# Two of four recurrent mixers take a block's 512 tokens at once; outputs after all states

## The chip, the core and the metric

The kernel runs on one core of a Trainium2 chip. The metric is the device time of one execution, in microseconds (us), lower is better. Each core has a matrix engine, TensorE (PE in the rows; PEld is its loading of weights, which overlaps the matmuls), the elementwise engines VectorE (DVE), ScalarE (ACT) and GpSimd (POOL), and SyncE (SP), which issues the DMA transfers here. PSUM is the memory that TensorE writes, SBUF the one that it reads.

## The reference

Two layers of a decoder. Each layer projects its input (2048 prompt tokens of width 1024, and 64 sample tokens that ride along) into four head groups, runs a recurrence in each, projects back, and adds a cross-attention into 256 memory tokens. Three of the groups (retention, HGRN2 and GLA) share one recurrence, in the reference's words:

```python
# S_t = diag(exp g_t) S_{t-1} + k_t v_t^T,  o_t = S_t^T q_t
o, s_ret  = chunked_gated_linear(q, k, v, log gamma, st['ret'])     # retention, 4 heads, 64 x 64 state
o, s_hgrn = chunked_gated_linear(silu(q), k_h, i, log_f, st['hgrn']) # HGRN2,     4 heads, 64 x 64
o, s_gla  = chunked_gated_linear(q, k, v, log_a, st['gla'])          # GLA,       4 heads, 32 x 64
o, S_rwkv = rwkv7_scan(r, w, k, v, kk, a, s0)                        # RWKV-7
out = concatenate([o_ret, o_hgrn, o_gla, o_rwkv]) @ w_out
```

Each group's output is normalised per head and gated with silu(g). The outputs are the tokens after both layers, the final states, and the memory keys and values.

## The kernel before

**Tiling.** The 2048 prompt tokens are four blocks b of TB = 512 tokens, each of NT = 4 tiles of 128. The eight steps (l,b) of two layers run one after the other in `block()`; the samples ride in b = 0 (`smp`), with their own mixers placed in blocks 0 and 1 (`TURN`).

**One block.** In program order: the projections of RWKV; `R_rwkv` in two halves of 256 tokens (PSUM lanes `psa` and `psc`); the projections of GLA, then `R_gla` in two halves (lane `psb`); the projections of HGRN, then `R_hgrn` in two halves (lane `psb`); the projections of retention, then `R_ret` in two halves (`psa`, `psc`). After it `gates()` multiplies with silu(g) (`th`, line 1266), and `finish()` does the output projection, the cross-attention and, with the next block's tokens, the normalisation and its transposes (`xs`, line 430, matmuls psb<-fpack,xs). Dense matmuls, those against the 1024-wide weights, write to lane `psd`; their weights come in 1 MB pieces into a ring `whl` of three. Weights that are still raw come through a ring `wrp` of three (tag "w", tiles `wraw`), which is in use in blocks 0 and 1 and idle in 2 and 3. Every PSUM lane has two buffers.

**A gated-linear mixer.** `dyadic()` builds the scores inside a tile of 128 tokens level by level, s = 1, 2, 4, 8, 16, 32, 64. At each level `products()` is a run of small matmuls of q against k on `psb`, whose results DVE puts into the score tile `sT` (line 736, a copy under a mask); then DVE scales k (`k_step`) and q (`q_step`) by the decays so far, and POOL forms the next decays `tot`. In GLA, where two heads share 64 partitions, q is held twice, masked (`qx`). `totok()` transposes the decayed k to tokens (`gmn` in GLA, `ha` in HGRN, `rkd` is retention's). `outputs()` then goes tile by tile: the query against the state (psb<-S_gla,qx), the scores against v (psb<-dn_gv,sT), the sum of kᵀv (psb<-dn_gv,gmn), and the update of the state in place on DVE (line 624); only then the next tile. At its end the whole output `osb` is normalised (`head_norm`) and transposed (psa or psc <-fpack,osb).

**Order.** Each engine runs its list in order. The list is made from priorities by program order, with an offset for each named part (`PRI`, so `wk2`, the GLA mixer, is pulled 223 ahead); `held()` keeps matmuls together, 12 dense ones or 48 others, before another lane may come between. So on TensorE dense runs stand between the small runs of the mixers, and whatever dense work is still unread covers the mixers' waits for DVE; late in a block none is left.

A program's small fp32 matmul is recorded twice in the trace: x16 in an order listing is x32 in a timeline row.

Of the kernel before, what the change touches and what calls it, by code (L numbers as in the profile page):

```python
# [22 lines left out]
TB = 512  # L23
# [110 lines left out]
def decoder(ctx, tc, I, C, O):  # L134
# [5 lines left out]
    NH = 4  # L140
# [422 lines left out]
    class Seg:  # L563
        def __init__(self, sample):
            self.sample = sample
            self.P = SN if sample else 128
            self.nt = 1 if sample else 2
            self.n = self.P * self.nt
            self.levels = SLEVELS if sample else LEVELS
# [26 lines left out]
    def outputs(seg, sT, at, v, qd, S, NG, NC, kT, tot, wp, eps, center, evac, state_out=None):  # L596
# [5 lines left out]
        if not seg.sample:  # L602
            po = PS("r").rearrange("p (t n) -> p t n", t=2)
            p5 = po.rearrange("p t (c g j d) -> p t c g j d", c=NC, g=2, j=NP)
            es = [slice(0, 64), slice(64, 128)]
            for t in range(nt):
                for c in range(NC):
                    for j in range(NP):
                        for e in es:
                            mm(p5[e, t, c, :, j, :], qd[:, c, j, t * 128 + e.start:t * 128 + e.stop], S[:, c, :], True, False)  # L610
                        for g in range(2):
                            h = c * NG + g * NP + j
                            x = sT[:, at(t, h)].rearrange("p e n -> p (e n)")
                            for e in es:
                                mm(po[e, t, h * 64:(h + 1) * 64], x[:, e], v[:, t, h * 64:(h + 1) * 64], False, True)
                pu = PS("r")[:, :NC * 64].rearrange("p (c n) -> p c n", c=NC)
                for h in range(NH):
                    c, g = divmod(h, NG)
                    mm(pu[g * KD:(g + 1) * KD, c, :], kT[:, t, h * KD:(h + 1) * KD], v[:, t, h * 64:(h + 1) * 64])
                for c in range(NC):  # L620
                    for p in range(2):
                        gs = slice(64 * p, 64 * p + 64)
                        blk = S[gs, c, p * 64:(p + 1) * 64]
                        V.scalar_tensor_tensor(blk, blk, tot(t, c)[gs], pu[gs, c, :], ALU.mult, ALU.add)
            tags = ("rqT", "rkT", None) if center else ("qx2", "qx2", 2)
            o = wp.tile([128, 2, 256], F32, name="osb", tag=tags[0], bufs=tags[2])
            A.activation(o, po, AF.Copy)
            head_norm(o, 128, 2, eps, center, wp, tags[1:], evac)
# [30 lines left out]
    def place(NG, NC, nt):  # L659

        NP = NG // 2

        def at(t, h):
            c, g = divmod(h, NG)
            p, j = divmod(g, NP)
            return ((p * nt + t) * NC + c) * NP + j
        return at

    def dyadic(seg, q, k, a, NG, NC, sT, wp):
# [10 lines left out]
        mine = lambda x, p: x[:, p * w:(p + 1) * w]  # L680

        def apart(i):
            if NP == 1:
                return q.unsqueeze(2)
# [6 lines left out]
        def products(s, f):  # L691
# [10 lines left out]
            for p in range(2):  # L702
                yield (mine(sT[:P], p)[:, :, 0, :].rearrange("p u (b f s) -> p u b f s", f=2, s=s)[:, :, :, f, :],
# [7 lines left out]
        def q_step(s, tot, x):  # L711
# [5 lines left out]
            new = wp.tile([128, NC, n // (2 * s)], F32, name=f"tot{s}", tag=f"tot{s}")  # L717
# [9 lines left out]
        tt(V, q, q, a, ALU.mult)  # L727
        tot = q_step(1, a, q.unsqueeze(2))
        Q[0] = apart(1)
        for li, s in enumerate(seg.levels):  # L730
# [6 lines left out]
            else:  # L737
                A.activation(sT[64:128, :, 1, :], sT[64:128, :, 0, :], AF.Copy)
                G.memset(sT[64:128, :, 0, :], 0.0)
                ps = [PS("r")[:, :NC * NP * 64].rearrange("p (c g n) -> p c g n", c=NC, g=NP) for _ in range(2)]  # L740
                for c in range(NC):
                    for t in range(nt):
                        for p in range(2):
                            mm(ps[p][64 * t:64 * t + 64, c], k[rows[p], c, t * P:t * P + 64], Q[0][rows[p], c, :, t * P + 64:t * P + 128])
                for t in range(nt):
                    for p in range(2):
                        o = mine(sT[0:64], p)[:, t * NC * NP:(t + 1) * NC * NP, 1, :]
                        A.activation(o, ps[p][64 * t:64 * t + 64].rearrange("p c g n -> p (c g) n"), AF.Copy)
# [4 lines left out]
        return Q[0], tot  # L753
# [18 lines left out]
    def gain(on, col):  # L772
        def f(ps):
            A.activation(on, ps, AF.Copy, scale=col)
        return f

    def plain(on):
        def f(ps):
            A.activation(on, ps, AF.Copy)
        return f  # L780

    def R_gla(l, seg, st, d, on, wp):
        c = cols[l]
        n = seg.n
        qk, v, sm = d["qk"], d["v"], d["sm"]
# [12 lines left out]
        sT = wp.tile([128, seg.nt * NH, seg.P // 64, 64], F32, name="sT", tag="sT")  # L798
        qd, tot = dyadic(seg, qk[:, 0:1, :], qk[:, 1:2, :], a, 4, 1, sT, wp)
        at = place(4, 1, seg.nt)  # L800
        kT = totok(qk[:, 1:2, :], 1, seg, wp, "gmn", 128)
        if seg.sample:
# [4 lines left out]
            outputs(seg, sT, at, v, qk[:, 0:1, :], S, 4, 1, kT, decay, wp, 32 * RMS_EPS, False,  # L807
                    gain(on, c["gla_norm"][:, 0:1]), lambda: sample_state_out(S, O[7][l], 32))
        else:
            outputs(seg, sT, at, v, qd, st, 4, 1, kT, lambda t, cc: tot[:, cc, t:t + 1], wp, 32 * RMS_EPS, False,  # L810
# [1211 lines left out]
```

## Time and profile before

| | |
|---|---|
| runs | 3624.22, 3611.39, 3616.11 us; median 3616.11 us |
| the profiled execution | 3606.43 us, its span 3604.6 us, so 1.8 us around it |
| mean granted TensorE clock | 0.968 of full |
| busy | PE 3366.3 us (93%), DVE 2112.9 (59%), ACT 1274.3 (35%), POOL 553.0 (15%) |
| idle time of PE in front of its matmuls | 227.8 us in all |

The profiled execution is 9.7 us under the median. The page's first part gives the busy time of each engine as a share of the span. The chain of waits starts at the last instruction and goes back to whatever released each step. The table of waits gives, for one engine, what it waited for, the total, the number of times and the longest. The timeline merges consecutive instructions of one kind into a row: its start, its length, how many, and in brackets the idle time ahead with what ended it. As matmuls are pipelined, the cost of a run in such a row is better read from the start of the next row than from its own length.

### The profile page before, as it was taken

How to read it: one execution, taken by the hardware profiler on the slowest of the kernel's cores; microseconds unless marked ns; L12 is line 12 of the kernel's file. 1: busy time of each engine (PE TensorE's matmuls, PEld its weight loads, DVE VectorE, ACT ScalarE, POOL GpSimd, SP SyncE). 2: the span in 40 equal slices, each digit the busy share in tenths (PEclk: the TensorE clock that was granted, in tenths of full speed). 3: DMA queues.
4: the chain of work that ended last, by engine and by line, in shares of the span. 5: the costliest groups of instructions: out<-in, count | busy, mean ns of one | idle time of the engine just before them, and what ended most of it. 6: DMA issues, size and time to landing. Idle time of an engine off the chain costs nothing.

```text
span 3604.6 us, 85661 instructions
## 1 busy us (share of the span) xinstructions
PE 3366.3 (93%) x36138; PEld 2835.7 (79%) x36138; DVE 2112.9 (59%) x6047; ACT 1274.3 (35%) x2729; POOL 553.0 (15%) x680
## 2 busy tenths in 40 slices
PE   7998799998999999999999997999889999999998
PEld 5877688886978888888877866878678888878887
DVE  5677545675436754576446765467644567446754
ACT  4442334422243324332344332443213333244323
POOL 3323231020000100011122242111100011000100
PEclk9999899998999999999999997999989999999999
DMA  6522565235662254324453255542445522542255
GB/s 191 184 98 89 180 218 192 77 112 163 200 215 90 82 196 150 135 76 173 170 172 121 83 155 175 197 153 94 136 153 186 176 98 92 188 160 103 76 195 188
DMA packets 241957, 530.79 MB, mean 147 GB/s; under 512 B 66854, under 2 KB 179750, under 8 KB 197542
## 3 DMA queue, kind: packets, MB, share of 16 engines
q1 hardware_dynamic: 241574, 525.31, 42.5%
q8 instruction: 285, 4.67, 0.5%
q14 instruction: 98, 0.80, 0.1%
HBM read 410.10 MB, written 115.16 MB: 146 GB/s over the span
## 4 chain that ended last, share of the span: by engine, by line
PE 75%; DVE 12%; ACT 5%; issue 3%; DMA 3%; POOL 2%; SPq 0%; POOLq 0%; ACTq 0%; DVEq 0%
PE psd L221 39%; PE psc L221 13%; PE psa L221 11%; PE psb L221 6%; PE psa L263 2%; PE psb L263 2%; PE psc L263 2%; DVE rsq L227 1%; DMA wraw<-in_w_in 1%; POOL whl L227 1%; DVE osb L227 1%; DVE hri L283 1%; DVE hss L552 1%; DVE dn_hq L227 0%; DMA whl<-w_low 0%
## 5 line engine op out<-in xcount | busy, mean ns | idle before, releaser
L221 PE MATMUL psd<-act,whl 128*128 128x512 f32 (+1 forms) x4032 | 1008.5, 402 | 28.6 <-DVE th L1266 12.8
L221 PEld LDWEIGHTS psd<-act,whl 128*128 128x128 f32 (+1 forms) x4032 | 741.4, 189 | 203.5 <-DVE th L1266 15.3
L221 PE MATMUL psd<-whl,act 128*128 128x256 f32 x3840 | 541.4, 292 | 7.0 <-POOL whl L227 3.3
L221 PEld LDWEIGHTS psd<-whl,act 128*128 128x128 f32 x3840 | 482.9, 193 | 28.6 <-issue 9.2
L227 POOL TENSOR_TENSOR whl<-wraw,whl 128x1024 fp32r<-128x1024 f32 (+1 forms) x90 | 218.0, 2428 | 383.3 <-ACT whl L349 366.2
L271 POOL TENSOR_TENSOR ri<-ri,mhalf 128x1 f32<-128x1 f32 (+1 forms) x87 | 50.6, 582 | 1103.9 <-DVE ri L270 1065.3
L221 PE MATMUL psd<-whl,oh 128*128 128x256 f32 x1152 | 211.4, 284 | 0.0
L221 PEld LDWEIGHTS psd<-whl,oh 128*128 128x128 f32 x1152 | 177.4, 189 | 0.9 <-issue 0.3
L221 PE MATMUL psd<-whl,ol 128*128 128x256 f32 x576 | 162.8, 283 | 0.0
L349 ACT ACTIVATE whl<-wraw 128x1024 fp32r<-128x1024 f32 (+1 forms) x90 | 94.0, 1048 | 120.9 <-DMA wraw<-in_w_in 40.5
L932 ACT ACTIVATE Xb<-X 32x256 f32<-32x256 f32 (+1 forms) x164 | 67.6, 412 | 166.0 <-DVE X L951 119.9
L221 PEld LDWEIGHTS psd<-whl,ol 128*128 128x128 f32 x576 | 108.5, 188 | 1.0 <-DVE ol L227 1.0
L736 DVE COPY_PREDICATED sT<-upack,psb 128x128 f32<-128x128 uint8 x320 | 89.6, 327 | 33.2 <-PE psb L221 31.5
L227 DVE TENSOR_TENSOR x<-x,psd 128x256 f32<-128x256 f32 x72 | 30.3, 421 | 132.1 <-PE psd L221 132.1
L221 PEld LDWEIGHTS psb<-dn_hq,dn_hf 64*64 64x64 f32 x3840 | 73.9, 135 | 29.5 <-issue 13.9
L221 PE MATMUL psb<-dn_hq,dn_hf 64*64 64x32 f32 (+1 forms) x3840 | 89.2, 223 | 8.0 <-DVE dn_hf L821 3.0
L1266 DVE SCALAR_TENSOR_TENSOR th<-th,psd 128x512 f32<-128x512 f32 x48 | 32.3, 686 | 109.1 <-ACT th L1265 109.1
L426 ACT ACTIVATE xs<-xn 128x1024 f32<-128x1024 f32 (+1 forms) x34 | 35.8, 1053 | 165.8 <-PE psb L263 153.2
L221 PEld LDWEIGHTS psd<-hts,wraw 128*64 128x64 f32 x1984 | 68.8, 144 | 18.9 <-issue 9.6
L221 PE MATMUL psa<-whl,oh 128*128 128x256 f32 x448 | 82.7, 282 | 0.0
L221 PE MATMUL psc<-whl,oh 128*128 128x256 f32 x448 | 82.6, 282 | 0.0
L221 PE MATMUL psd<-hts,wraw 128*64 128x64 f32 x1984 | 78.8, 232 | 3.8 <-DVE th L1266 3.8
(760 smaller groups left out, 6972.5 us busy)
## 6 DMA issues: line engine op xcount, KB each, us to landing
whl<-w_w_out SPq DMA_DIRECT2D x56, 1024.0 KB
wraw<-in_w_in SPq DMA_DIRECT2D x76, 512.0 KB
wraw<-in_w_out SPq DMA_DIRECT2D x32, 512.0 KB
w_w_out<-whl SPq DMA_DIRECT2D x16, 1024.0 KB
x<-x SPq DMA_DIRECT2D x32, 512.0 KB
whl<-w_rw_r SPq DMA_DIRECT2D x12, 1024.0 KB
whl<-w_rw_k SPq DMA_DIRECT2D x12, 1024.0 KB
whl<-w_rw_v SPq DMA_DIRECT2D x12, 1024.0 KB
```

The source lines that it names most:

```text
L221: PE.matmul(out, lhsT=lhsT, rhs=rhs, start=start, stop=stop, skip_group_check=True)
L227: e.tensor_tensor(out, a, b, op)
L263: PE.transpose(out, in_, ident[:rows, :rows])
L271: G.tensor_tensor(y, y, mhalf[:P], ALU.pow)
L283: V.scalar_tensor_tensor(y, t, 1.5, y, ALU.add, ALU.mult)
L349: A.activation(hl[:, 0], raw, AF.Copy)
L426: A.activation(out, xt, AF.Square, accum_out=ss[:P])
L552: V.tensor_reduce(ss[:P, :n4], sq[:P, :n4], AX.X, ALU.add)
L736: V.copy_predicated(out, bc(mk, [P, w, 32 // s, s]), ps)
L932: A.activation(dst(b), src(b), AF.Copy)
L1266: V.scalar_tensor_tensor(th, th, 1.0, x, ALU.add, ALU.mult)
```

## The change

In the six blocks without samples (b = 1, 2, 3 of both layers) GLA and HGRN run once over 512 tokens (`Seg(False, 4)`) in place of two halves of 256; block 0 keeps its halves. The products, the masked copies, `k_step` and `q_step` so have the double width. The scores become two tiles, one for each half of the partitions, and the intermediate states get a tile `Sx`; where a mixer takes 512 tokens, these three come from the ring `wrp`, elsewhere from the mixer's own pool. `outputs()` has a new order, for retention too and in all eight blocks: first the sums kᵀv of all tiles into one PSUM buffer, then DVE moves the state from St[t] to St[t+1] instead of in place, then all outputs, in pairs of tiles. GLA's q is written to its two masked copies by ACT when it leaves PSUM (`apart`, a scale by the mask `hm32`), and not by DVE at each mixer; its k lies in the ring `th`, which the gates and silu use too. The decays `tot` take two tags in turn instead of one for each level.

```diff
-    def outputs(seg, sT, at, v, qd, S, NG, NC, kT, tot, wp, eps, center, evac, state_out=None):
+    def outputs(seg, score, v, qd, S, NG, NC, kT, tot, wp, eps, center, evac, state_out=None):
         if not seg.sample:
-            po = PS("r").rearrange("p (t n) -> p t n", t=2)
+            if nt > 2:
+                x = wrp.tile([128, nt - 1, NC, 128], F32, name="Sx", tag="w")
+            else:
+                x = wp.tile([128, nt - 1, NC, 128], F32, name="Sx", tag="Sx")
+            G.memset(x, 0.0)
+            St = [S] + [x[:, t] for t in range(nt - 1)] + [S]
+            pu = PS("r")[:, :nt * NC * 64].rearrange("p (t c n) -> p t c n", t=nt, c=NC)
             for t in range(nt):
...
-                pu = PS("r")[:, :NC * 64].rearrange("p (c n) -> p c n", c=NC)
                 for h in range(NH):
-                    mm(pu[g * KD:(g + 1) * KD, c, :], kT[:, t, h * KD:(h + 1) * KD], v[:, t, h * 64:(h + 1) * 64])
+                    mm(pu[g * KD:(g + 1) * KD, t, c, :], kT[:, t, h * KD:(h + 1) * KD], v[:, t, h * 64:(h + 1) * 64])
+            def move(t):
...
-                        V.scalar_tensor_tensor(blk, blk, tot(t, c)[gs], pu[gs, c, :], ALU.mult, ALU.add)
+                        a, b = (y[gs, c, p * 64:(p + 1) * 64] for y in St[t:t + 2])
+                        V.scalar_tensor_tensor(b, a, tot(t, c)[gs], pu[gs, t, c, :], ALU.mult, ALU.add)
+            for t in range(nt - 1):
+                move(t)
+            for t0 in range(0, nt, 2):
+                po = PS("r").rearrange("p (t n) -> p t n", t=2)
+                for t in range(t0, t0 + 2):
...
+                                mm(p5[e, t - t0, c, :, j, :], qd[...], St[t][:, c, :], True, False)
+                                    mm(po[e, t - t0, h * 64:(h + 1) * 64], x[:, e], v[:, t, h * 64:(h + 1) * 64], False, True)
+            move(nt - 1)
...
     def dyadic(...)
+        if nt > 2:
+            sT = [wrp.tile([128, w, nh, 64], F32, name="sT", tag="w") for p in range(2)]
...
     def block(...)
+        parts = [slice(0, TB)] if not smp else [slice(0, TB // 2), slice(TB // 2, TB)]
+        gr = Seg(False, NT // len(parts))
-        qk = op.tile([128, 2, TB], F32, name="dn_qk", tag="on_hgrn")
+        gq = op.tile([128, 1, 2, TB], F32, name="dn_gq", tag="on_hgrn")
+        gk = dnp.tile([128, 1, TB], F32, name="dn_gk", tag="th", bufs=2)
+        def apart(ps):
+            for j in range(2):
+                A.activation(gq[:, 0, j, :], ps, AF.Copy, scale=K["hm32"][:, j:j + 1])
-        for hb in range(2):
-            with within("wk2", hb, 2), on_lane("b"), right("wk2") as wp:
-                R_gla(l, pr, st["gla"], dict(qk=h2(qk, hb), ...), h2(on["gla"], hb), wp)
+        for x in parts:
+            with within("wk2"), on_lane("b"), right("wk2") as wp:
+                R_gla(l, gr, st["gla"], dict(q=gq[:, :, :, x], k=gk[:, :, x], ...), on["gla"][:, :, x], wp)
```

`R_hgrn` is called likewise. In the whole program TensorE has 25,186 matmuls for 25,192, DVE 5,633 instructions for 6,049, ACT 2,438 for 2,512 (among them 25 loads of a function table for 37), POOL 645 for 685, SP 855 as before; what TensorE does falls into 5,967 runs of one kind for 6,409. Of the dense runs there are 57 fewer, and of the products 56 fewer in HGRN and 46 fewer in GLA.

**The products.** TensorE, HGRN's levels beside RWKV's inversion (Xb, Wb, X) in layer 0, block 2. `psb<-dn_hq,dn_hf` are the products, `psd<-whl,act` dense work. Before:

```order
L221 MATMUL psb<-dn_hq,dn_hf 64x32 x16
L221 MATMUL psd<-whl,act 128x256 x12
L221 MATMUL psc<-Wb,XB 32x128 x8
L221 MATMUL psb<-dn_hq,dn_hf 64x32 x16
L263 MATMUL psa<-fpack,X 128x128 x2
L221 MATMUL psd<-whl,act 128x256 x12
L221 MATMUL psc<-Xb,XB 32x128 x8
L221 MATMUL psb<-dn_hq,dn_hf 64x32 x16
L221 MATMUL psd<-whl,act 128x256 x12
L221 MATMUL psa<-Wb,XB 32x128 x8
```

The same engine and place, after:

```order
L221 MATMUL psb<-dn_hq,dn_hf 64x32 x32
L221 MATMUL psd<-whl,act 128x256 x24
L263 MATMUL psa<-fpack,X 128x128 x2
L221 MATMUL psc<-Xb,XB 32x128 x8
L221 MATMUL psb<-dn_hq,dn_hf 64x32 x32
L221 MATMUL psd<-whl,act 128x256 x12
L221 MATMUL psa<-Wb,XB 32x128 x8
L221 MATMUL psd<-whl,act 128x256 x12
L263 MATMUL psc<-fpack,X 128x128 x2
L221 MATMUL psb<-dn_hq,dn_hf 64x32 x32
```

Two runs of products became one of twice the length, and some runs of 12 dense matmuls joined into 24.

**States and outputs.** TensorE, the end of HGRN in the same block: `ha` is k as tokens, so psb<-dn_hv,ha is the sum kᵀv; psb<-S_hgrn,dn_hq reads the state. Before, the first half:

```order
L221 MATMUL psb<-S_hgrn,dn_hq 64x128 x2
L221 MATMUL psb<-dn_hv,sT 64x64 x4
L221 MATMUL psb<-dn_hv,ha 64x64
L221 MATMUL psb<-S_hgrn,dn_hq 64x128
L221 MATMUL psb<-dn_hv,ha 64x64
L221 MATMUL psb<-S_hgrn,dn_hq 64x128
L221 MATMUL psb<-dn_hv,ha 64x64
L221 MATMUL psb<-dn_hv,sT 64x64
L221 MATMUL psb<-dn_hv,ha 64x64
L221 MATMUL psb<-dn_hv,sT 64x64 x3
```

After, from the start of the mixer's output:

```order
L221 MATMUL psb<-dn_hv,ha 64x64 x16
L221 MATMUL psb<-S_hgrn,dn_hq 64x128 x2
L221 MATMUL psb<-dn_hv,sT 64x64 x4
L221 MATMUL psb<-S_hgrn,dn_hq 64x128 x2
L221 MATMUL psb<-dn_hv,sT 64x64 x4
L221 MATMUL psd<-whl,act 128x256 x3
L221 MATMUL psb<-Sx,dn_hq 64x128 x2
L221 MATMUL psb<-dn_hv,sT 64x64 x4
```

The four sums kᵀv of all tiles stand in one run at the front, the outputs are no longer broken by them, and later tiles read `Sx`.

**The end of a block.** TensorE, retention's second half at the end of layer 0, block 1; psb<-fpack,xs belongs to the next block's normalisation, `osb` to the outputs, psd<-act,whl and psd<-hts,wraw are dense. Before:

```order
L221 MATMUL psd<-act,whl 128x512 x12
L263 MATMUL psa<-fpack,dn_rq 128x128 x4
L263 MATMUL psb<-fpack,xs 128x128 x12
L263 MATMUL psc<-fpack,osb 128x128 x4
L263 MATMUL psc<-fpack,dn_rk 128x128 x4
L221 MATMUL psc<-rqT,rkT 128x128 x4
L221 MATMUL psc<-dn_rv,rkd 64x64 x4
L221 MATMUL psa<-rqT,rkT 128x128 x4
```

After:

```order
L221 MATMUL psd<-act,whl 128x512 x24
L221 MATMUL psd<-hts,wraw 64x64 x16
L263 MATMUL psb<-fpack,xs 128x128 x4
L263 MATMUL psa<-fpack,osb 128x128 x4
L263 MATMUL psa<-fpack,dn_rk 128x128 x4
L221 MATMUL psd<-act,whl 128x512 x4
L221 MATMUL psa<-rqT,rkT 128x128 x4
L221 MATMUL psd<-act,whl 128x512 x8
L221 MATMUL psc<-rqT,rkT 128x128 x4
L221 MATMUL psc<-dn_rv,rkd 64x64 x8
```

Eight of the twelve transposes of `xs` now stand earlier in the list, dense work stands ahead of the rest and within the half, and 12 more dense matmuls stand ahead of the block's last transposes of `osb`. In layer 1, block 2 the transposes of `xs` stand behind 36 dense matmuls and the last `osb`, with 96 dense ones behind them. In layer 1, block 1 the end of the block still has no dense work.

On SP the loads of raw weights for the gates of block 1 (two `wraw<-in_w_in`) now wait for a buffer that HGRN's `sT` and `Sx` hold, and they stand ahead of the issue of two of the `whl` pieces of retention; before, they were issued early in the block.

## Rows read from the trace of the kernel before

**Rows 1.** The page: busy time, share of the span and instructions

```profile
PE 3366.3 (93%) x36138; PEld 2835.7 (79%) x36138; DVE 2112.9 (59%) x6047; ACT 1274.3 (35%) x2729; POOL 553.0 (15%) x680
```

**Rows 2.** The page: the chain that ended last, by engine

```profile
PE 75%; DVE 12%; ACT 5%; issue 3%; DMA 3%; POOL 2%; SPq 0%; POOLq 0%; ACTq 0%; DVEq 0%
```

**Rows 3.** Waits of PE: line and releaser, us in total, times, longest

```profile
PE psc L263 <- DVE osb L227: 30.0, 7, 6.8
PE psb L263 <- DVE xs L430: 27.9, 7, 6.0
```

**Rows 4.** Windows: length, busy of PE, PEld, DVE, ACT, POOL, PEclk, DMA

```profile
885.00:1302.00 417.00, 410.16 (x4470) 346.15 (x4469) 229.03 (x689) 138.43 (x307) 30.79 (x59) 1.00 0.45 151
...
850.00:886.00 36.00, 20.78 (x154) 17.35 (x153) 23.26 (x62) 9.02 (x16) 2.15 (x3) 0.57 0.35 122
```

**Rows 5.** Timeline of PE, HGRN's levels: start, length, runs

```profile
798.56 0.67 PE L221 MATMUL psb<-dn_hq,dn_hf 64*64 64x32 f32 x32
799.16 1.70 PE L221 MATMUL psd<-whl,act 128*128 128x256 f32 x12
800.78 0.67 PE L221 MATMUL psb<-dn_hq,dn_hf 64*64 64x32 f32 x32
...
803.01 0.46 PE L221 MATMUL psb<-dn_hq,dn_hf 64*64 64x64 f32 x16
803.40 0.86 PE L221 MATMUL psd<-whl,act 128*128 128x256 f32 x5
```

**Rows 6.** Timeline of PE, a dense run of 24

```profile
760.92 3.14 PE L221 MATMUL psd<-whl,act 128*128 128x256 f32 x24
764.03 0.66 PE L263 MATMUL psa<-fpack,wosb 128*128 128x128 f32 x4
```

**Rows 7.** Timeline of PE, the outputs of one half of GLA

```profile
1499.03 0.44 PE L221 MATMUL psb<-S_gla,qx 128*64 128x128 f32 x4
...
1499.71 0.30 PE L221 MATMUL psb<-dn_gv,gmn 128*32 128x64 f32 x2
1499.94 0.43 PE L221 MATMUL psb<-S_gla,qx 128*64 128x128 f32 x2
...
1501.99 1.20 PE L221 MATMUL psd<-act,whl 128*128 128x512 f32 x4
1503.11 0.32 PE L221 MATMUL psb<-dn_gv,gmn 128*32 128x64 f32 x8
1503.36 2.11 PE L221 MATMUL psd<-act,whl 128*128 128x512 f32 x8
...
1505.97 0.44 PE L221 MATMUL psb<-S_gla,qx 128*64 128x128 f32 x4
...
1506.47 0.39 PE L221 MATMUL psb<-S_gla,qx 128*64 128x128 f32 x4
```

**Rows 8.** Groups of DVE by shape: busy us, mean ns | idle before

```profile
L736 DVE COPY_PREDICATED sT<-upack,psb 128x128 f32<-128x128 uint8 x320 | 89.6, 327 | 33.2 <-PE psb L221 31.5
L951 DVE COPY_PREDICATED X<-upack,psa 128x256 f32<-128x256 uint8 x32 | 14.3, 446 | 25.1 <-PE psa L221 24.6
L227 DVE TENSOR_TENSOR dn_hf<-dn_hf,tot 128x256 f32<-128x256 f32 x96 | 47.9, 499 | 3.5 <-PE psb L221 2.3 <-issue 0.7
L227 DVE TENSOR_TENSOR qx<-dn_qk,fpack 128x512 f32<-128x512 f32 x32 | 22.0, 689 | 13.2 <-PE psb L263 9.8 <-ACT dn_qk L1270 2.8
L624 DVE SCALAR_TENSOR_TENSOR S_hgrn<-S_hgrn,tot,psb 64x64 f32<-64x64 f32 x128 | 35.7, 279 | 22.0 <-PE psb L221 19.1
```

**Rows 9.** Timeline of PE, ends of blocks (0,1) and (1,2)

```profile
857.36 1.09 PE L263 MATMUL psb<-fpack,xs 128*128 128x128 f32 x4 [5.28 <-DVE xs L430]
...
877.33 1.09 PE L263 MATMUL psc<-fpack,osb 128*128 128x128 f32 x4 [6.82 <-DVE osb L227]
...
3079.95 1.97 PE L263 MATMUL psb<-fpack,xs 128*128 128x128 f32 x8 [5.96 <-DVE xs L430]
```

**Rows 10.** The chain in order of time: a weight piece between dense runs

```profile
2965.47 5.77 DMA whl<-w_ret_k
```

More of the change, by code (lines that the diff above doesn't have):

```diff
@@ L679, in dyadic, with score @@
         rows = [slice(64 * p, 64 * p + 64) for p in range(2)]
-        mine = lambda x, p: x[:, p * w:(p + 1) * w]
+        if nt > 2:
+            sT = [wrp.tile([128, w, nh, 64], F32, name="sT", tag="w") for p in range(2)]
+        else:
+            sT = [wp.tile([128, w, nh, 64], F32, name="sT", tag=f"sT{p}") for p in range(2)]
+        def score(t, h):
+            c, g = divmod(h, NG)
+            p, j = divmod(g, NP)
+            return sT[p][:P, (t * NC + c) * NP + j].rearrange("p e n -> p (e n)")
         def apart(i):
-            if NP == 1:
-                return q.unsqueeze(2)
+            if NP == 1 or not seg.sample:
+                return q if len(q.shape) == 4 else q.unsqueeze(2)
             x = wp.tile([128, NC, NP, n], F32, name="qx2", tag="qx2", bufs=2)
@@ L716, in q_step @@
             tt(V, qv[:, :, :, 1, :], qv[:, :, :, 1, :], d, ALU.mult)
-            new = wp.tile([128, NC, n // (2 * s)], F32, name=f"tot{s}", tag=f"tot{s}")
+            size, turn = max(n // (2 * s), 1), (len(bin(s)) + 1) % 2
+            new = wp.tile([128, NC, n // 2 >> turn], F32, name=f"tot{s}", tag=f"tot{turn}")[:, :, :size]
             tt(G, new, tv[:, :, :, 0], tv[:, :, :, 1], ALU.mult)
@@ L726, in dyadic @@
             tt(V, out, ps, bc(K["pmask"][:P].unsqueeze(1).unsqueeze(3), [P, w, 32, 1]), ALU.mult)
-        tt(V, q, q, a, ALU.mult)
-        tot = q_step(1, a, q.unsqueeze(2))
+        if len(q.shape) == 4:
+            tt(V, q, q, bc(a.unsqueeze(2), list(q.shape)), ALU.mult)
+        else:
+            tt(V, q, q, a, ALU.mult)
+        tot = q_step(1, a, q if len(q.shape) == 4 else q.unsqueeze(2))
         Q[0] = apart(1)
@@ L752, in dyadic @@
             tt(V, q, Q[0][:, :, 0], Q[0][:, :, 1], ALU.add)
-        return Q[0], tot
+        return score, Q[0], tot
     def sample_state(src, nm, wp, KD):
@@ L772, in gain, with f @@
     def gain(on, col):
[L773 to L774 removed]
+        def f(ps, o=0):
+            A.activation(on[:, :, o:o + ps.shape[2]], ps, AF.Copy, scale=col)
         return f
     def plain(on):
[L778 to L779 removed]
+        def f(ps, o=0):
+            A.activation(on[:, :, o:o + ps.shape[2]], ps, AF.Copy)
         return f
@@ L797, in R_gla @@
         a = az.unsqueeze(1)
[L798 to L801, printed above, removed]
+        score, qd, tot = dyadic(seg, q, k, a, 4, 1, wp)
+        kT = totok(k, 1, seg, wp, "gmn", 128)
         if seg.sample:
@@ L821, in R_hgrn @@
             V.tensor_scalar(f[:, i], f[:, i], c["mc1"][:, i:i + 1], c["c1"][:, i:i + 1], ALU.mult, ALU.add)
-        sT = wp.tile([128, seg.nt * NH, seg.P // 64, 64], F32, name="sT", tag="sT")
-        qd, tot = dyadic(seg, q, f, a, 2, 2, sT, wp)
-        at = place(2, 2, seg.nt)
+        score, qd, tot = dyadic(seg, q, f, a, 2, 2, wp)
         kT = totok(f, 2, seg, wp, "ha", 256)
@@ L860, in R_ret @@
         sT = wp.tile([128, seg.nt * NH, seg.P], F32, name="sT", tag="sT")
-        at = lambda t, h: t * NH + h
+        score = lambda t, h: sT[:P, t * NH + h]
         for t0 in range(0, nt, step):
@@ L1423, in block @@
             proj_t("hg_i", lambda ps, t0: copy_ps(hv[:, t0:t0 + 2, :], ps), hvs)
-        for hb in range(2):
-            with within("wk3", hb, 2), on_lane("b"), right("wk3") as wp:
-                R_hgrn(l, pr, st["hgrn"], dict(q=h2(hq, hb), f=h2(hf, hb), v=t2(hv, hb)), h2(on["hgrn"], hb), wp)
+        for x in parts:
+            with within("wk3"), on_lane("b"), right("wk3") as wp:
+                R_hgrn(l, gr, st["hgrn"], dict(q=hq[:, :, x], f=hf[:, :, x], v=hv[:, tiles(x)]), on["hgrn"][:, :, x], wp)
         rank("D_ret")
```

85 lines of the change are left out of this document (41 added, 44 removed).

## The prediction, written before the changed kernel ran

> **What bounds the kernel now.** I read the page first. PE is busy 93% of the span, the next engine, DVE, 59% [rows 1], and three quarters of the chain that ended last are PE's own work [rows 2]. So a change pays where it shortens PE's list, or where it fills one of PE's waits; 227.8 us of the span are such waits. The windows show that there are two kinds of stretch. In the middle of a block PE is busy 410.16 of 417.00 us at full clock, and DVE only 229.03 [rows 4]: the waits are already covered, and what counts is how long PE's list is. At the end of a block dense work has run out: from 850 to 886 us PE is busy 20.78 of 36.00 us and the granted clock is 0.57 of full, so that even its own work takes about twice as long [rows 4]. The table of waits names what PE waits for there: for `osb`, 30.0 us in 7 waits on one lane alone, and for `xs`, 27.9 us in 7 [rows 3].
>
> The change makes PE's list shorter in runs and hardly in matmuls (6 of 25,192 fewer). So the question of the sum is what a run costs beside its matmuls, and I take that from the timeline, always from the start of a run to the start of the next.
>
> **Part by part.** All terms are for the whole program; the six blocks with b = 1 to 3 change, the other two hardly.
>
> *Products of GLA and HGRN.* A run of 32 small matmuls takes 799.16 − 798.56 = 0.60 us, a run of 16 takes 803.40 − 803.01 = 0.39 us [rows 5]. The second is of 64 columns and the first of 32, so it isn't the same shape, but if both followed one line, a matmul would cost 0.21/16 = 0.013 us and the run itself 0.60 − 32 × 0.013 = 0.18 us. Sixteen pairs of runs in each of six blocks become one run each: 96 × 0.18 = 17 us saved. The bound from below is nothing: if 0.60/32 = 0.019 us is what each matmul costs, joining saves none.
>
> *The sums kᵀv and the outputs.* In GLA the sum kᵀv comes in twos, and two cost 1499.94 − 1499.71 = 0.23 us where eight in a row cost 1503.36 − 1503.11 = 0.25 us [rows 7]. That is the clearest sign of a price by run. The first tile's output, broken by those twos, takes 1501.99 − 1499.03 = 2.96 us [rows 7], where an unbroken pair of state read and scores takes 1506.47 − 1505.97 = 0.50 us and a tile needs two, so 1.0 us [rows 7]. One half so costs about 2.96 + 0.25 + 1.0 = 4.2 us and a block 8.4. After, a block needs eight pairs, 4.0 us, and 32 matmuls of kᵀv, between 0.45 us (one price by run) and 1.0 us (four times 0.25): 4.5 to 5.0. Saved: 3.4 to 3.9 us a block, some 21 us in six. HGRN's sums are not so dear in a run and I give it 0.5 us a block, 3 us. Together **24 us**, between 15 and 27.
>
> *Other joined runs.* Retention's kᵀv loses one run in each of 16 halves, the transposes to tokens a few: some 28 runs by the same 0.18 us, 5 us.
>
> *Dense runs.* 57 fewer, since with fewer small runs between them runs of 12 become 24. A run of 12 takes 800.78 − 799.16 = 1.62 us [rows 5], one of 24 takes 764.03 − 760.92 = 3.11 us [rows 6]: 2 × 1.62 − 3.11 = 0.13 us a run, 57 × 0.13 = 7 us.
>
> *Ends of blocks.* In (0,1) PE waits 5.28 us for `xs` and in (1,2) 5.96 us [rows 9]. After the change the transposes of `xs` stand earlier or behind dense work and behind the last `osb`, as the listing shows. Both waits should go: 11 us. What is late next is `osb` (6.82 us at 877.33 [rows 9]): it now has 12 dense matmuls ahead, about 3 us of that wait. The stretch of 36 us is at 0.57 of the clock, and 20.78 busy us at that clock are about 12 at full [rows 4]; filled with dense work it should keep the full clock for some two thirds. I take 8 us for both blocks. Together **22 us**, between 8 (the dense work stands there but the clock falls as before, and one of the `xs` waits comes back) and 30. The end of (1,1) stays uncovered, and I give it nothing.
>
> *What the wider steps give back.* At a level DVE now copies two score tiles of twice the width, and multiplies k and q at twice the width. Before: 2 × 0.33 for the copies, 0.50 for k of HGRN, as much for q: 1.65 us a half [rows 8]. The 128x256 copy under a mask costs 0.45, a 128x512 multiply 0.69 [rows 8]: 2 × 0.45 + 2 × 0.69 = 2.3 us for the whole, instead of 3.3 for two halves. DVE has less to do, but a step from products to products is longer by 0.65 us, and only 12 or 24 dense matmuls (1.62 or 3.11 us) and a run or two of RWKV's stand between. I let half of GLA's eight steps in each block wait 0.5 us: 6 × 4 × 0.5 = 12 us. The moves of the state go out of the way of the outputs but all stand before the second one: three tiles by four instructions of 0.28 us [rows 8] in HGRN, 3.4 us, beside outputs of the first tile (1.0 us) and three dense matmuls (0.4 us); TensorE may wait some 0.7 us a block, 4 us. The new copies of q on ACT, which replace four of 0.69 us a block on DVE [rows 8] (32 in all), and the zeroing of `sT` and `Sx` on POOL, lie beside dense work on engines that are busy 35% and 15% [rows 1], and I put them at nothing; without that cover a step would lose about 0.7 us a block. The score tiles in the ring of raw weights hold up two loads in block 1 and what stands behind them on SP, two pieces of `whl`: 4 us, since one such piece takes 5.77 us [rows 10]. In all **20 us** given back, between 5 and 60.
>
> Sum: 17 + 24 + 5 + 7 + 22 − 20 = 55 us. The profiled execution took 3606.43 us, so 3551; it lay 9.7 us under the median of the three, so against the median of 3616.11 it is 3561. I say **3560 us**.
>
> **The rivals.** *TensorE pays by the matmul.* Then joining products and dense runs brings nothing, and of the sum remain 24 + 22 − 20 = 26 us, and about 3 of the small runs: 3587 us. For it speaks that 0.019 us a matmul explains the run of 32 as well; against it the twos of kᵀv, and that the run of 16 costs 0.024 us a matmul [rows 5]. The Trainium skill, page "TensorE: Matmul & The Clock Gate", section "Wait — 56ns, not 53.3ns?", has a floor of about 25 ns from start to start of matmuls, however small, which agrees with the run of 16 and not with the run of 32 or with two in 0.23 us. By that floor alone nothing that is joined would save anything, the sums kᵀv neither, and 22 − 20 = 2 us would be left: 3614 us; since the twos speak against it, that has 0.03 of this rival's chance.
>
> *DVE becomes the bound of a step.* In the stretch where RWKV's inversion runs beside the products, DVE has both to do, and the chain from products to products is now in one piece where two halves used to take turns: while one half waited for DVE, PE had the other lane's work. If each of the 16 steps a block waits, the change loses as soon as a wait is over (17 + 24 + 5 + 7 + 22 − 8)/96 = 0.7 us, the 8 being the moves and the loads, that aren't part of it. At 1 us, between the 0.65 by which a step is longer and the whole 2.3, it would be 96 − 67 = 29 us slower: 3645 us. For it: the row of products has 31.5 of its 33.2 idle us by PE [rows 8], so DVE follows at once and is not far ahead; against it: DVE's work falls by 1 us of 3.3 per level and it is busy 229 of 417 us there [rows 4].
>
> *The loads turn up late.* With fewer small runs between, dense work eats its weights faster: three transitions a block, in six blocks, where a piece that takes 5.77 us [rows 10] could be late by up to 2 us, 36 us in all, with the rest of the sum intact: 3596 us. Against it: waits for `whl` by DMA are not among PE's long ones now. For it: SP issues in order, and waits on a busy ring hold all behind.
>
> **How the numbers follow.** The forecast has 0.64, TensorE by the matmul 0.15, late loads 0.09, DVE as the bound 0.12. The forecast's own spread is 3520 to 3600 (the bounds above, not all at one end); the rivals of 3587 to 3600 lie within it or close. I take 3518 to 3605, which leaves out the slower case and a little on either side. A measurement of this kernel tells about 0.3%, 11 us, from no change. Faster by over 0.3% (under 3605): all of the forecast but a little, most of the two mild rivals, 0.80. Within: 0.09. Slower by over 0.3%: 0.11.
>
> **What would show it.** In the profile after: runs of 64 products that take about 1.0 us and not 1.2 (the price by run), 16 or 32 sums kᵀv of GLA in a row at 0.45 to 1.0 us, and a block's outputs of GLA near 5 us. In the table of waits `xs` falls by some 11 us and `osb` keeps more than half of its 30.0 us on psc. The stretch from 850 us has a granted clock over 0.57. Waits for `dn_hf`, `dn_gk` or `dn_hq` on psb, now small, grow to 10 or 20 us; if they come to over 60, DVE is the bound. Wrong would be: PE's busy time falls by less than 20 us; new waits of psd for `whl` by DMA of over 10 us; or the end of (1,1), uncovered in both, gets longer because the outputs now wait for all moves.

## The result: 0.8% slower

The changed kernel takes 3643.22 us (median of 4 runs, 3640.04 to 3651.97), the kernel before 3615.78 us; the ratio is 1.0082, its 95% interval 1.0068 to 1.0097. The prediction was 3560 us, between 3518 and 3605. The profiled execution has a span of 3639.7 us.

The page of the changed kernel, busy times and the chain by engine, which answer to [rows 1] and [rows 2]:

```profile
PE 3361.5 (92%) x36126; PEld 2844.2 (78%) x36126; DVE 2072.8 (57%) x5631; ACT 1255.1 (34%) x2655; POOL 536.3 (15%) x640
...
PE 70%; DVE 15%; issue 5%; ACT 4%; DMA 3%; POOL 2%; SPq 0%; POOLq 0%; ACTq 0%; DVEq 0%
```

PE's busy time hardly moved, 3366.3 to 3361.5 us, which looks as if the merged runs had saved nothing. But at half clock (a granted clock of 0.5, the 1.2 GHz level) a matmul counts nearly twice as long as busy: four transposes of 128x128 have 1.11 us at 2182.93 us in the changed kernel, at half clock, and 0.60 at 2059.41 us in the kernel before, at full clock. So I split the span of each profile: from each matmul's start to the next one's, less the idle time ahead of the next; of what lies in stretches whose granted clock is 0.5, half is "lost to half clock", the rest "work at full clock". Half is an estimate: a run of 32 products, below, takes 1.01 us for 0.60 and not twice as long.

| us | span | PE waits | lost to half clock | work at full clock |
|---|---|---|---|---|
| before | 3604.6 | 222.1 | 80.6 | 3285.3 |
| changed | 3639.7 | 262.1 | 137.9 | 3223.3 |

The remaining 16 to 17 us of a span lie ahead of its first matmul and behind the start of its last.

**The work fell by 62 us; waits rose by 40 and the loss to half clock by 57.** By blocks, cut where ACT takes the first small projection of each (`sm`): the two blocks b = 0, which the change does not widen, went from 1035.8 to 1079.3 us, and the six others only from 2528.4 to 2519.5. The windows of the blocks (0,0) and (1,0), of before and then of the changed kernel (columns as in [rows 4]), show it by the clock:

```profile
40.40:547.30 506.90, 454.88 (x5110) 382.90 (x5109) 304.92 (x807) 190.65 (x371) 159.93 (x125) 0.95 0.48 160
1776.90:2305.80 528.90, 476.74 (x5152) 394.83 (x5151) 306.69 (x830) 202.61 (x416) 144.68 (x120) 0.94 0.45 150
```

```profile
40.80:573.50 532.70, 468.96 (x5108) 395.31 (x5107) 309.13 (x803) 192.14 (x376) 160.28 (x134) 0.91 0.44 149
1802.00:2348.60 546.60, 487.72 (x5153) 402.50 (x5152) 303.70 (x826) 204.38 (x421) 144.59 (x129) 0.89 0.42 143
```

Inside (1,0) the place stands out in the timeline of PE. Before, HGRN's second half has dense runs between its products:

```profile
2063.78 0.67 PE L221 MATMUL psb<-dn_hq,dn_hf 64*64 64x32 f32 x32
2064.38 3.14 PE L221 MATMUL psd<-whl,act 128*128 128x256 f32 x24
2067.45 0.67 PE L221 MATMUL psb<-dn_hq,dn_hf 64*64 64x32 f32 x32
```

In the changed kernel both halves of HGRN come some 133 us later after the block's start (in (0,0) some 120). The first half, of which rows follow, stands with the sample's mixers and no dense run at all from 2135 to 2200 us, at a clock of 0.53 (the window's row stands last):

```profile
2181.51 1.08 PE L221 MATMUL psb<-dn_hq,dn_hf 64*64 64x32 f32 x32 [1.68 <-DVE hri L283]
...
2183.97 1.08 PE L221 MATMUL psb<-dn_hq,dn_hf 64*64 64x32 f32 x32
2186.40 1.08 PE L221 MATMUL psb<-dn_hq,dn_hf 64*64 64x32 f32 x32 [1.35 <-DVE dn_hq L227]
```

```profile
2135.00:2200.00 65.00, 52.06 (x575) 34.49 (x574) 35.70 (x112) 12.52 (x28) 18.62 (x29) 0.53 0.24 66
```

The same run of 32 products is 0.67 us long before and 1.08 here, and two of these three wait for DVE.

### The profile page after: what moved, and what is told of

It reads as the page before. It is cut to its first block, busy times and chain, and to the rows that moved or that the text cites. A ratio compares the mean times of both kernels' runs of the same rounds, so it can differ in the third digit from the quotient of the medians.

```text
span 3639.7 us, 85145 instructions
## 1 busy us (share of the span) xinstructions
PE 3361.5 (92%) x36126; PEld 2844.2 (78%) x36126; DVE 2072.8 (57%) x5631; ACT 1255.1 (34%) x2655; POOL 536.3 (15%) x640
## 4 chain that ended last, share of the span: by engine, by line
PE 70%; DVE 15%; issue 5%; ACT 4%; DMA 3%; POOL 2%; SPq 0%; POOLq 0%; ACTq 0%; DVEq 0%
PE psd L221 38%; PE psc L221 12%; PE psa L221 11%; PE psb L221 5%; PE psb L263 2%; PE psc L263 2%; PE psa L263 2%; DMA wraw<-in_w_in 1%; DVE rsq L227 1%; POOL whl L227 1%; DVE Sx L622 1%; DVE hss L552 1%; DVE sT L755 1%; ACT Xb L949 1%; DVE osb L227 0%
## 5 line engine op out<-in xcount | busy, mean ns | idle before, releaser
L221 PE MATMUL psd<-act,whl 128*128 128x512 f32 (+1 forms) x4032 | 1018.7, 405 | 23.6 <-DVE th L1283 8.1
L221 PEld LDWEIGHTS psd<-act,whl 128*128 128x128 f32 (+1 forms) x4032 | 752.2, 191 | 206.8 <-issue 22.3
L221 PEld LDWEIGHTS psd<-whl,act 128*128 128x128 f32 x3840 | 487.2, 195 | 38.6 <-issue 16.3
L349 ACT ACTIVATE whl<-wraw 128x1024 fp32r<-128x1024 f32 (+1 forms) x90 | 94.2, 1048 | 103.4 <-DMA wraw<-in_w_in 34.1
L221 PEld LDWEIGHTS psb<-dn_hq,dn_hf 64*64 64x64 f32 x3840 | 77.4, 151 | 40.4 <-issue 27.9
L227 POOL TENSOR_TENSOR tot<-tot 128x8 f32<-128x8 f32 (+7 forms) x128 | 37.5, 293 | 424.4 <-DVE dn_gq L227 179.1
L755 DVE COPY_PREDICATED sT<-upack,psb 128x256 f32<-128x256 uint8 (+1 forms) x200 | 76.7, 429 | 34.3 <-PE psb L221 32.8
```

The costliest lines, as they stand in the source:

```text
L221: PE.matmul(out, lhsT=lhsT, rhs=rhs, start=start, stop=stop, skip_group_check=True)
L227: e.tensor_tensor(out, a, b, op)
L349: A.activation(hl[:, 0], raw, AF.Copy)
L755: V.copy_predicated(out, bc(mk, [P, w, 32 // s, s]), ps)
```

## Experiments

Each is timed beside the kernel before, on the same chip; ratios are to it.

**Why block 0? 32 bytes of SBUF.** As the built programs place their tiles, the RWKV sample's pool reserves a partition's bytes up to 216064. HGRN's scratch pool grows down towards it: it begins at 216544 before and, with the new tile `Sx`, at 216032 in the changed kernel. It so shares 32 bytes with a pool that is released only when the RWKV sample is through, and HGRN's first tile, `ha`, waits for that: in (1,0) it is first written at 1995.1 us before and at 2153.5 in the changed kernel.

```diff
-                x = wp.tile([128, nt - 1, NC, 128], F32, name="Sx", tag="Sx")
+                x = wp.tile([128, nt - 1, NC, 128], F32, name="Sx", tag="Sx" if center else "qx2", bufs=None if center else 2)
```

> The changed kernel, but in blocks with halves the intermediate state Sx shares the slots of osb and hsq (tag qx2) and has no room of its own. HGRN's scratch pool then begins at byte 217056 of a partition and not at 216032; the pool of the RWKV sample ends at 216064, so in the changed kernel they share 32 bytes. Theory (those 32 bytes make HGRN of block 0 wait until the RWKV sample is through, and it then runs without dense work beside it): the waits (+18 us) and the half clock (+43 us) that the changed kernel has more in block 0 of both layers go, 3643 - 61 = 3582 us, between 3570 and 3595, and HGRN's products of block 0 stand again right behind GLA. Rival (GLA's k in the ring th, or the outputs after all states, delay block 0): no change, 3643 within 8. Rival (DVE is the bound of the wider steps): no change either, since blocks 1 to 3 keep them.

Measured: 3621.96 us, ratio 1.0017 (0.9999 to 1.0035). `ha` is back at 1997.5 us. The two blocks b = 0 fell by 32 us, from 1079.3 to 1047.6, and the others have 8 more in this profile (2519.5 to 2527.7). Some 23 us by the ratios (0.0065), not 61: the overlap is one cause, and others were beside it. To see it alone, the kernel before with an unused tile in HGRN's pool:

```diff
         a = wp.tile([128, 2, n], F32, name="ha", tag="ha")
+        if not seg.sample:
+            pad = wp.tile([128, 120], F32, name="pad", tag="pad")     # e3: 128 in place of 120
...
```

> The kernel before, with 480 unused bytes a partition in HGRN's scratch pool: it then begins at 216064, right where the pool of the RWKV sample ends. Every theory expects the time of before, 3616 us within 8; if what counts is the pool of the block's end (to 216112), which this one overlaps, it would already be slower by 10 us or more.

> The kernel before, with 512 unused bytes in HGRN's scratch pool, 32 more than in the other: it begins at 216032 as in the changed kernel and shares 32 bytes with the pool of the RWKV sample. Nothing else differs. Theory of the 32 bytes: slower by 40 to 70 us, 3656 to 3686 us, with HGRN's products of block 0 at half clock behind the RWKV sample. Rivals: 3616 within 8.

Measured: 3613.46 us, ratio 0.9992 (0.9978 to 1.0006), and 3656.95 us, ratio 1.0122 (1.0105 to 1.0139). Thirty-two unused bytes more cost 43 us, 31 of them in the two blocks b = 0 (1041.3 to 1072.5). Timelines of PE, first with 480 bytes, then with 512:

```profile
2072.42 0.67 PE L221 MATMUL psb<-dn_hq,dn_hf 64*64 64x32 f32 x32
2073.02 1.70 PE L221 MATMUL psd<-whl,act 128*128 128x256 f32 x12
...
2075.17 0.67 PE L221 MATMUL psb<-dn_hq,dn_hf 64*64 64x32 f32 x32
```

```profile
2181.31 1.08 PE L221 MATMUL psb<-dn_hq,dn_hf 64*64 64x32 f32 x32 [1.68 <-DVE hri L283]
...
2183.77 1.08 PE L221 MATMUL psb<-dn_hq,dn_hf 64*64 64x32 f32 x32
2186.21 1.08 PE L221 MATMUL psb<-dn_hq,dn_hf 64*64 64x32 f32 x32 [1.35 <-DVE dn_hq L227]
```

The second is the changed kernel's picture, in a kernel that has nothing else of the change.

**What is the width worth?** From here on all kernels have the 32 bytes cleared. First, halves in all blocks, then the width in one mixer only:

```diff
-        parts = [slice(0, TB)] if not smp else [slice(0, TB // 2), slice(TB // 2, TB)]
+        parts = [slice(0, TB // 2), slice(TB // 2, TB)]
```

> As the first, but GLA and HGRN take halves of 256 tokens in all blocks; the order of outputs (all states first), q split by ACT and k in the ring th stay. What it has less than the first is the taking of 512 tokens at once. If a run of products costs 0.18 us by itself, some 96 runs and the joined dense runs come back: 20 to 25 us slower than the first, about 3605. If the wider steps cost as much in waits as they save in runs, the same as the first within 8 us. If DVE is the bound of the wider steps, faster than the first by 10 us or more.

> As e1_clear, but HGRN takes halves in all blocks and only GLA takes 512 tokens. e1_clear is 32 us slower than e4_halves, where both take halves. HGRN's steps are the wider ones (a copy, k and q at 128x256 to 128x512) and two thirds of the cost should be HGRN's: 3600 us here, 10 above e4_halves. If GLA is at fault, 3615 or more; if widening GLA pays by its runs, below 3588.

> As e1_clear, but GLA takes halves in all blocks and only HGRN takes 512 tokens. By the same split 3612 us, 22 above e4_halves; if the two add up, this one and e6_gla_whole lie together 32 us above twice e4_halves.

Measured: halves 3589.99 us (ratio 0.9930, 0.9914 to 0.9946), GLA alone at 512 tokens 3589.36 (0.9936, 0.9920 to 0.9953), HGRN alone 3596.39 (0.9958, 0.9943 to 0.9973), both, in e1_clear, 3621.96. So the width gains nothing. By these times it costs little in one mixer and 31 us in both: the two do not add up, and my guess that HGRN has two thirds of the cost fell. The blocks of the profiles are less clear. Blocks 1 to 3, the only ones in which these four differ, take 2496.2 us with halves, 2501.5 with GLA wide, 2517.5 with HGRN wide and 2527.7 with both: 5, 21 and 31 us more, nearly a sum, and HGRN the dearer. The two blocks b = 0, whose matmuls stand in almost the same order in all four, take 1054.1, 1043.6, 1039.9 and 1047.6 us. So blocks move by up to 14 us without a cause in the edit, and whether the two mixers add up stays open. The same split of the span:

| us | span | PE waits | lost to half clock | work at full clock |
|---|---|---|---|---|
| e1_clear, both at 512 | 3616.5 | 256.7 | 116.4 | 3226.8 |
| e6, GLA at 512 | 3586.3 | 239.3 | 100.0 | 3230.4 |
| e7, HGRN at 512 | 3598.6 | 236.3 | 111.4 | 3234.4 |
| e4, halves | 3590.6 | 225.1 | 102.8 | 3246.1 |

The width does save 19 us of work and pays 32 in waits and 14 in clock. Rows of the waits led me first to RWKV: in e1_clear PE waits for the small steps of its inversion, 20 us in blocks 1 to 3 where e4_halves has 2, as if the wide DVE instructions stood ahead of them. So DVE's part was cut in two again:

```diff
-            tt(V, qv[:, :, :, 1, :], qv[:, :, :, 1, :], d, ALU.mult)
+            for y in cuts(n // (2 * s)):        # two halves where nt > 2; the copies of scores and k likewise
+                z = qv[:, :, y, 1, :]
+                tt(V, z, z, bc(tv[:, :, y, 0:1], list(z.shape)), ALU.mult)
```

> As e1_clear, but where a mixer takes 512 tokens, DVE's work at a level (the copies of scores under a mask, the scaling of k and of q) is issued in two instructions of half the width, as it was with halves; TensorE's runs of products stay whole. Theory (the wide DVE instructions stand ahead of the short steps of RWKV's inversion, so that TensorE waits for Xb, Wb and X, 20 us in e1_clear against 2 us in e4_halves): some of these waits go, 5 to 20 us faster than e1_clear (3622), with waits of psa and psc for Xb under 8 us. Rival (what delays RWKV is that a level's step as a whole is longer, however it is cut): no faster than e1_clear, or slower by some 5 us for the more instructions.

Measured: 3619.62 us, ratio 1.0020 (1.0005 to 1.0036), no faster. Waits of PE in e1_clear, then in e5_split:

```profile
PE psc L221 <- DVE Xb L947: 4.9, 5, 1.3
...
PE psa L221 <- ACT Xb L949: 4.4, 9, 0.5
PE psc L221 <- ACT Xb L949: 4.2, 9, 0.5
```

```profile
PE psa L221 <- ACT Xb L956: 3.9, 10, 0.5
...
PE psc L221 <- ACT Xb L956: 2.4, 6, 0.5
```

The waits in these lines fell from 13 us to 6, and PE's waits in all stayed, 256.7 and 257.6: they came back elsewhere. That theory was wrong; DVE's instruction width is not what bounds the time. The rival, that a level's step as a whole is longer however it is cut, fits the result; nothing here tests it further.

**Where the waits stand.** I sorted PE's waits of blocks 1 to 3 by stage. Ahead of HGRN's first product, from GLA's first on: 6.7 us before, 18.8 in the changed kernel, 18.4 in e1_clear, 7.5 in e4_halves. What is new there is the waits for RWKV's inversion (1.6 us before, 13.9 in the changed kernel), and GLA's width brings them: the stage waits 17.1 us in e6 and 7.2 in e7. From HGRN's last output to ten us after retention's last scores: 30.7, 47.1, 48.3, 24.1 (23.6 in e6, 37.4 in e7). The second is the larger, but it begins where HGRN ends, so it is also longer where HGRN ends early: 196, 489, 492 and 133 us in the six blocks together. From HGRN's first product to the block's end, the same work in all, the waits are 94, 102, 105 and 86 us: 8 us more than before and 19 more than with halves, not 16 and 24. How early the mixers end is in the windows. GLA's and HGRN's products in (1,1), in e1_clear and then in e4_halves:

```profile
2396.40:2432.70 36.30, 33.98 (x561) 27.91 (x560) 27.26 (x66) 13.79 (x31) 3.47 (x9) 1.00 0.26 89
2476.80:2524.20 47.40, 43.78 (x870) 39.90 (x872) 40.93 (x97) 14.06 (x31) 8.04 (x14) 1.00 0.26 96
```

```profile
2381.80:2460.60 78.80, 78.52 (x1090) 65.30 (x1090) 49.14 (x160) 31.45 (x70) 8.29 (x23) 1.00 0.24 85
2482.90:2561.10 78.20, 75.97 (x1355) 65.86 (x1354) 55.67 (x187) 22.45 (x52) 13.75 (x26) 1.00 0.32 103
```

A mixer at 512 tokens needs half as many turns, so it is through in 36 and 47 us where halves take 79 and 78; DVE is busy 86% in the second where it was 71%. Its work is gone early, and my reading is that nothing of it is then left to lie beside retention at the end of the block. That was tested by moving HGRN alone, by its priority (`wk3`, line 41):

```diff
-'wk3': -38
+'wk3': 120        # e14: 250
```

> As e1_clear (3622 us), but the priority of HGRN's mixer (wk3) is 120 in the place of -38: its products start some 60 to 100 dense matmuls later in a block, and its outputs end at dense matmul 426 to 492 and not 345 to 436. Theory (with both mixers at 512 tokens they are through early, and retention's stage then has no mixer's work and little dense work to cover its waits, 48 us against 24 in e4_halves): waits in retention's stage fall to 30 to 40 us and the time to 3600 to 3614. Rival (the wide steps cost by themselves, wherever they stand): 3622 within 6.

> As e1_clear, but with a priority of 250: HGRN's outputs end at dense matmul 576 to 768, beside retention or behind it. Theory: waits of retention's stage fall below 30 us in blocks 1 to 3; HGRN's own products then stand where dense work is out in blocks 0 and 2, which costs again, so the time is between 3600 and 3640 and the gain lies in blocks of b = 1. Rival: as e1_clear in the blocks b = 1.

Measured: 3578.44 us, ratio 0.9903 (0.9875 to 0.9932), and 3664.98 us, 1.0146 (1.0118 to 1.0173). At 120 the waits of retention's stage fell from 48.3 to 32.0 us, as expected, but half of that came back in the other stages: all waits of blocks 1 to 3 fell by 8 us (131.3 to 123.4), and what these blocks lose to half clock by 7. The time fell by more than expected: the six blocks by 15 us, and (1,0) by another 21, which the theory does not speak of. At 250 retention's stage waits 10.3 us, but HGRN's own stage 65.4. The blocks b = 1 gain 9 us on e1_clear, as expected, but blocks 2 and 3 lose 56, so that the time is above what I had expected: there HGRN has been moved to where dense work is out. So the place matters, in both directions, and takes away 15 of the 31 us that the width costs in blocks 1 to 3. That the offsets written into the kernel had been right for halves is not shown: halves with a moved HGRN were not run.

**The raw weights' room, and block 1.**

```diff
-        parts = [slice(0, TB)] if not smp else [slice(0, TB // 2), slice(TB // 2, TB)]
+        parts = [slice(0, TB)] if b > 1 else [slice(0, TB // 2), slice(TB // 2, TB)]     # e9
...
-            if nt > 2:
+            if raw[0] and not center:        # e10, halves: Sx, and sT likewise, from wrp in blocks 1 to 3
                 x = wrp.tile([128, nt - 1, NC, 128], F32, name="Sx", tag="w")
```

> As e1_clear, but GLA and HGRN take 512 tokens in blocks 2 and 3 only, where the ring of raw weights is idle; in block 1, where raw weights go through it for the sample's gates and output projection, they take halves. By the blocks of the profiles, e1_clear is 22 us longer than e4_halves in the two blocks b = 1 and 10 us in the four later ones. Theory (the scores in the raw weights' room and the wide steps cost where block 1 has the sample's mixers and raw loads as well): 3622 - 22 = 3600 us, within 6. Rival (the width costs alike in all six blocks): 32 x 4/6 above e4_halves, 3611. Rival (only the wide mixers next to each other in any block matter, and block 1 was chance): 3618 or more.

> As e4_halves (3590 us), nothing is taken at 512, but in blocks 1 to 3 the score tiles and Sx lie in the ring of raw weights as in the changed kernel. Nothing else differs. Theory (the raw room is what costs in block 1, since its three buffers are just the three tiles of a mixer, and raw loads and mixers wait for each other): 12 to 22 us slower than e4_halves. Rival (the width of the steps costs, not the room): within 6 us of e4_halves.

Measured: 3601.44 us, ratio 0.9968 (0.9950 to 0.9986), and 3599.28 us, 0.9958 (0.9944 to 0.9971). Without the width in block 1 some 18 us come back, as expected. The room by itself costs 10 us (0.0028), between my two expectations, and in the profile block 1 has it (860.5 us in e4_halves, 874.1 here; blocks 2 and 3 1635.7 and 1632.5). So part of what the width costs in block 1 is the room that its tiles take, and not its steps.

**The order "first all states".** Halves again, with the outputs of the kernel before:

> As e4_halves, but the outputs stand as in the kernel before: tile by tile, the state updated in place between them, in retention too. Theory (the order states first is what makes e4_halves faster than before, since kTv in one run of 16 and unbroken outputs save 24 us in blocks 1 to 3 and some 10 in block 0): 25 to 35 us slower than e4_halves, at the time of before, 3615 to 3625. Rival (q split by ACT, fewer decay tiles and k in the ring th bring it): 3590 to 3600.

Measured: 3605.87 us, ratio 0.9969 (0.9954 to 0.9985). The order is worth 14 us (0.0039), half of what I expected, the lesser rest of the change (q split by ACT, k in `th`, two tiles for scores) 11 against before. By the split, the order saves 37.5 us of work (3283.6 to 3246.1) and pays 16 in waits and 8 in clock. Most of that price is block 0: 1032.9 us in e8, 1054.1 in e4_halves (down to 1040 in other kernels here with nearly the same block 0); the other blocks gain, 2530.5 to 2496.2. Hence a version that uses each where it pays:

```diff
+            if tilewise[0]:              # set in block 0: outputs tile by tile, state in place
...
```

> A version put together from the others: block 0 has the outputs tile by tile as before (its two blocks took 1033 us in e8 and 1054 in e4_halves), the other blocks all states first; GLA takes 512 tokens in blocks 2 and 3, HGRN halves throughout. If the blocks add up, 3589 - 20 = 3569 us, 1.2% faster than before. If the blocks' gains are not their own (the order of one block moves the next), 3580 to 3595.

> As e11_mixed, but GLA takes halves in all blocks too. If taking 512 tokens of one mixer pays by its runs (16 us of PE's work in e6 against waits of 14), it is within 5 us of e11_mixed; if the joined runs pay fully where nothing else is wide, e11_mixed is 5 to 10 us faster.

> As e12_mixed_halves (3572 us: block 0 tile by tile, the others all states first), but GLA and HGRN take 512 tokens in blocks 1 to 3 and HGRN has the priority 120. If the early end explains the loss, 3575 to 3585; if the width costs by itself, 3572 + 32 = 3604 or more; if the 512 tokens pay by their runs once they are placed well, below 3565.

Measured: e11 3577.66 us (0.9898, 0.9879 to 0.9917), **e12 3571.60 us, ratio 0.9882 (0.9857 to 0.9906)**, the fastest of all, 1.2% under before and 2% under the changed kernel, so GLA's 512 tokens in blocks 2 and 3 gain nothing here either; e15 3599.81 us (0.9953, 0.9934 to 0.9971), between my cases. In the six wide blocks e15 is 6 us longer than e12 (2506 to 2500), so even placed later the 512 tokens gain nothing; the rest of its loss is (0,0) and (1,0), 1052 to 1034 us. HGRN's later place seems to do harm there together with the old outputs, since with the new ones, in e13, the two take 1027; no run takes this apart. Why (1,0) takes 513 us in e13 and 535 in e1_clear is not settled.

## Why the prediction was wrong

By the profiles the changed kernel lies 90 us above the 3551 of the sum: 43.5 in the two blocks b = 0, which the sum left out, and 46 in the six others, which gained 9 us and not 55.

- **Merged runs: right.** A run of 64 products takes 1.07 us, 1225.94 to 1227.01, and not twice the 0.60 of [rows 5]:

```profile
1225.94 1.14 PE L221 MATMUL psb<-dn_hq,dn_hf 64*64 64x32 f32 x64
1227.01 0.44 PE L263 MATMUL psc<-fpack,X 128*128 128x128 f32 x2
...
2952.94 0.63 PE L221 MATMUL psb<-dn_gv,gmn 128*32 128x64 f32 x32
2953.69 0.44 PE L263 MATMUL psc<-fpack,X 128*128 128x128 f32 x2
```

  In blocks 1 to 3 the products of both mixers went from 99.1 to 83.1 us: 16 saved, predicted 17. All sums kᵀv of GLA in one run take 0.75 us, predicted 0.45 to 1.0; with state reads and scores GLA's outputs went from 50.3 to 27.9 us, 22 saved, predicted 21; nearly all of that is the order, since e4_halves has 29 too. The rival by which TensorE pays by the matmul is out. The Trainium skill ("TensorE: Matmul & The Clock Gate", section "Wait — 56ns, not 53.3ns?") has a floor of about 25 ns from start to start. The trace does not agree: 64 recorded products in 1.07 us are 17 ns each, so that floor is not the whole price of these runs. All work: 62 us saved, 45 of them in blocks 1 to 3, where 53 were predicted, and 17 in block 0. My sign of being wrong, a fall of PE's busy time by less than 20 us, came (it fell by 4.8) and said nothing of the work, since busy time holds the half clock.
- **"The six blocks with b = 1 to 3 change, the other two hardly": the step that failed.** Block 0 got the new outputs and a larger scratch pool, and the list of the changed program, which was at hand, has HGRN's products there at dense matmul 1400 and not 924 of the program. I compared the lists only where the diff spoke of a wider mixer. 43.5 us of the miss: some 32 by the 32 bytes (e1 and e3), the rest beside the new outputs.
- **Ends of blocks: the place right, the sum wrong.** The end of (0,1) is now covered:

```profile
860.00:896.00 36.00, 30.16 (x310) 24.56 (x308) 23.34 (x78) 8.70 (x18) 2.40 (x4) 1.00 0.62 180
```

  30.16 us busy of 36.00 at full clock, where [rows 4] had 20.78 at 0.57. Waits for `xs` fell by the 11 us that I had named (27.9 to 16.7):

```profile
PE psc L263 <- DVE osb L227: 21.4, 6, 6.9
PE psb L263 <- DVE xs L430: 16.7, 5, 5.7
PE psb L263 <- DVE osb L227: 14.2, 7, 6.4
PE psa L263 <- DVE osb L227: 12.3, 4, 6.3
```

  The wait for `osb` behind the 12 dense matmuls is 3.93 us where it was 6.82, the 3 us that I had named. But the 8 us of clock did not come: in (0,1) 34.1 us lay at half clock before and 30.7 after, 17 of them now ahead of retention, between 794 and 815 us. And from HGRN's first product to the ends of blocks 1 to 3 PE waits 8 us more in all (94 to 102), while the loss to half clock in these blocks rose by 15 us (35.7 to 50.4). The 22 us came to about nothing.
- **What the wider steps give back: 12 us for GLA's steps came, by luck.** GLA's stage waits 12 us more (6.7 to 18.8), but not for GLA: in blocks 1 to 3 PE's waits for the inputs of both mixers' products stayed small (3.3 us before, 2.3 after). What grew in these blocks is the waits for RWKV's inversion (Xb, Wb and X), from 2 to 21 us. Those for Xb over the whole program, in the kernel before and then the largest three rows of the changed kernel:

```profile
PE psc L221 <- ACT Xb L932: 1.1, 4, 0.3
```

```profile
PE psc L221 <- DVE Xb L947: 4.9, 5, 1.3
PE psc L221 <- ACT Xb L949: 4.6, 10, 0.5
PE psa L221 <- ACT Xb L949: 4.4, 9, 0.5
```

  That is a cost on the inversion's lanes, where my sum had none. HGRN's stage waits no more than before (19.7, 16.3). The loads in the ring of raw weights had 4 us; with halves the room alone costs 10 (e10). What I had no term for is the inversion's waits, whose cause stays open after e5, that a mixer with fewer turns is a shorter cover, which e13 bears out for about half of the width's cost, and the half clock that stood beside the new waits.
- **The rival of DVE had the time (3645) and not the cause.** That it came so near is luck. It looked at the right stretch, since the new waits stand at RWKV's inversion beside the wide steps; but PE waits little for products, the split of DVE's instructions brought nothing, and 23 us of the loss are 32 bytes. The rival of late loads is out as it was put: waits of PE for `whl` by DMA stay at 2 us in all (2.4 before, 1.8 after).

## What to carry to other kernels

Before costing a change, lay the two lists side by side in the parts that it should *not* touch, and look at where each scratch pool begins: a pool that grows into another one moves whole stages, and no instruction count shows it. A longer run on the bounding engine is worth its saved starts only while the work that it shortens was no cover for something else; ask what will stand beside the next stage. Before reading a stage's waits, see that it has the same work in both kernels. With hand-set priorities a change of sizes is measured together with their places, so move one place before giving the sizes up.

## What the hardware showed

From two rows, an estimate: a run of these products costs some 0.13 us by itself (2 × 0.60 − 1.07) at full clock, beside 15 ns for each recorded product ((1.07 − 0.60)/32). Beside 40 us more of PE's waits the changed kernel has 57 us more lost to half clock. In (1,0) the granted clock is 0.5 for 61 us on end, from 2136 to 2197 us; PE has no dense run there, only small ones and short waits between them, the longest 1.73 us.
